# A transformer trunk in which every second weight unit of the down-projection gets its remainder from an adding DMA

## The chip, the cores and the metric

The kernel runs on one core of a Trainium2 chip. The metric is the device time of one execution in microseconds (us), and the median of several runs is compared. Engines are named as in the profile: PE is TensorE (PEld its weight loads), ACT is ScalarE, DVE is VectorE, POOL is GpSimd, and SP is the engine whose queue issues the loads. An engine's name with a q behind it (SPq) is its instruction queue.

## The reference

The reference is a decoder trunk of two layers over 256 tokens of width 2048 in 32-bit floating point. Each layer has an attention mixer with several kinds of heads, a cross-attention into 256 memory tokens, and a squared-ReLU MLP. The change touches the MLP alone, and of that the second product:

```python
def squared_relu_mlp(h, w_up, w_down):          # h (256, 2048)
    return jnp.square(jax.nn.relu(h @ w_up)) @ w_down   # w_up (2048, 8192), w_down (8192, 2048)

for l in range(DEPTH):                          # DEPTH = 2
    ...
    y = squared_relu_mlp(rms_norm(h, g_mlp_pre[l]), w_up[l], w_down[l])
    h = h + rms_norm(y, g_mlp_post[l])
```

## The kernel before

**The split.** Every large product is made from three matmuls. A 32-bit operand is split in two numbers of TensorE's fp32r format: a main part h, which is the operand rounded to fp32r, and a remainder l, which is the operand minus h, rounded likewise. `mm3` adds x_h·w_h, x_h·w_l and x_l·w_h in PSUM.

**Weight units.** Weights stream in from memory in units of two 128-row blocks by up to 512 columns, 512 KB each in the down-projection. A unit goes through three steps. `load` issues its DMA on SP into one of five raw buffers (`RAW = 5`). `convert` writes h on ScalarE (an activation with Copy) and l on VectorE (`tensor_sub` of raw and h), each into one of eight buffers (`WBUF = 8`). `gemm_a` uses h and l on TensorE. A unit of a matrix whose rows are scaled by a gain, the up-projection's among them, is converted in two halves of 512 columns with the gain multiplied in; the down-projection has no gain, so its units take one ScalarE and one VectorE instruction over 1024 elements per partition.

**The MLP.** For each layer, `mlp` runs four quarters q. A quarter has an up stage of four panels of 512 hidden columns (eight units each), whose outputs stay on chip as h and l of the hidden state, and a down stage of four panels of 512 output columns (again eight units each) that multiplies these 2048 hidden values by their rows of w_down and adds the result to y. A panel of the down stage holds two PSUM banks, one for each half of the tokens (tb), and a unit is used by twelve matmuls: two row blocks, two halves, three products. The last panel of the last quarter (q + p == 6) is worked in two passes, first all units for one half of the tokens, then all units for the other, so that the closing norm of the first half can run under the second. Its eight units are therefore in use through both passes.

**Order.** The program order is written out by the generator itself. `pump` places a conversion as soon as fewer than eight units are live, and `feed` places a load as soon as there are fewer than five unconverted ones; `track` keeps a clock for each engine from estimated durations, and these clocks decide where in the program each instruction stands. On the chip every engine runs its own instructions in that order and waits on semaphores: a conversion waits for its raw tile and for TensorE to be done with the unit eight places before, a load waits until the unit five places before has been converted, which is when raw is read no more.

**POOL** converts a few units of other matrices, updates one quarter of the residual at the end of a sub-layer (`UPD_POOL`), and works out some norms.

Of the kernel before, what the change touches and what calls it, by code (L numbers as in the profile page):

```python
# [15 lines left out]
AF = mybir.ActivationFunctionType  # L16
OP = mybir.AluOpType
# [43 lines left out]
class Unit:  # L61
    def __init__(self, dmas, nk, n, gains, passes):
        self.dmas, self.nk, self.n, self.gains, self.left = dmas, nk, n, gains, passes
        self.h = self.l = self.raw = None
        self.pool = False
        self.done_at = None


# [33 lines left out]
def blocks(ap):  # L102

    name = ap.tensor.name
    dims = list(ap.ap)
    o = ap.offset % dims[0][0] if dims[0][0] else ap.offset
    offs = [o]
    for step, num in dims[1:-1]:
        if step >= 64 and num > 1:
            offs = [x + step * i for x in offs for i in range(num)]  # L110
        else:
            dims[-1] = (dims[-1][0], dims[-1][1] + step * num // max(dims[-1][0], 1))
    last = (dims[-1][1] - 1) * dims[-1][0] if len(dims) > 1 else 0
    return {(name, b) for x in offs for b in range(x // 128, (x + last) // 128 + 1)}


class Gen:
# [9 lines left out]

    def __init__(self, ctx, tc, io):
        self.tc, self.nc, self.io = tc, Core(self, tc.nc), io
        self.clk = dict(pe=0.0, act=0.0, dve=0.0, pool=0.0, dma=0.0)  # L130
        self.rd, self.bank = {}, {}
        self.dep = 0.0
        self.seq = 0
        self.heap = []
        self.ready = set()
        self.units = []
        self.nconv = self.ndma = self.ncur = 0
        self.const = ctx.enter_context(tc.tile_pool(name="const", bufs=1))
        self.rawp = ctx.enter_context(tc.tile_pool(name="raw", bufs=self.RAW))
        self.wp = ctx.enter_context(tc.tile_pool(name="w", bufs=self.WBUF))  # L140
        self.xp = ctx.enter_context(tc.tile_pool(name="xt", bufs=4))
        self.tp = ctx.enter_context(tc.tile_pool(name="t", bufs=self.TB))
        self.sp = ctx.enter_context(tc.tile_pool(name="s", bufs=40))
        self.pp = ctx.enter_context(tc.tile_pool(name="ps", bufs=8, space=bass.MemoryType.PSUM))
        ctx.enter_context(tc.manual_schedule())
# [26 lines left out]
    def track(self, part, name, a, k):  # L172
        out = a[0]
        outs = [out] + ([k["accum_out"]] if "accum_out" in k else [])
        ins = [x for x in list(a[1:]) + [v for n, v in k.items() if n != "accum_out"] if isinstance(x, AP)]
        onchip = [x for x in ins if not str(x.space).endswith("DRAM")]
        n = out.free_size() if callable(out.free_size) else out.free_size
        psum = any(str(x.space).endswith("PSUM") for x in onchip)
        lat = 0.12
        if part == "pe":  # L180
            if name == "transpose":
                cost = max(n, 64) * 0.00085
            elif onchip[0].dtype == F32R:
                cost = n * (0.000425 if n >= 256 else 0.0017)
            else:
                cost = max(n, 128) * 0.00168
            lat = 0.2
        elif part == "act":
            cost = (0.03 if psum else 0.06) + n * 0.0009 + 0.093 * ("accum_out" in k) + \
                0.093 * isinstance(k.get("scale"), AP)  # L190
        elif part == "dve":
            if name == "tensor_reduce":
                n = onchip[0].free_size() if callable(onchip[0].free_size) else onchip[0].free_size
            two = 2 if name in ("tensor_scalar", "tensor_copy", "memset") and not psum else 1
            cost = 0.06 + n * 0.00115 / two
        elif part == "pool":
            cost = 0.12 + n * (0.0036 if name == "tensor_scalar" else 0.0023)
            lat = 0.15
        else:
            cost = max(n * 128 * 4 / 350e3, 0.4)  # L200
            lat = 2.0
        start = max([self.clk[part], self.dep] + [self.ready_at(x) for x in onchip])
        if part == "dma":
            start = max(start, self.clk["pe"] - 2.0)
        banks = {x.tensor.name for x in [*onchip, *outs] if str(x.space).endswith("PSUM")}
        for b in banks:
            who, when = self.bank.get(b, (part, 0.0))
            if who != part:
                start = max(start, when)
        end = start + cost  # L210
        self.clk[part] = end
        for b in banks:
            self.bank[b] = (part, end + lat)
        for x in outs:
            for b in blocks(x):
                self.rd[b] = end + lat
# [70 lines left out]
    def convert(self, u):  # L287
        nc = self.nc
        self.seq += 1
        u.h = self.wp.tile([128, 2, 512], F32R, tag="wh", name=f"h{self.seq}")  # L290
        u.l = self.wp.tile([128, 2, 512], F32R, tag="wl", name=f"l{self.seq}")
        n = u.n
        if self.nconv >= self.WBUF:
            self.dep = self.units[self.nconv - self.WBUF].done_at or 0.0
        if u.gains is None:
            a = slice(0, n)
            nc.scalar.activation(u.h[:, :, a], u.raw[:, :, a], AF.Copy)
            (nc.gpsimd if u.pool else nc.vector).tensor_sub(u.l[:, :, a], u.raw[:, :, a], u.h[:, :, a].bitcast(F32))
        else:
            for k in range(u.nk):  # L300
                g = self.gain_col(u.gains[k])
                nc.scalar.activation(u.h[:, k, :n], u.raw[:, k, :n], AF.Copy, scale=g)
                if u.pool:
                    nc.gpsimd.tensor_scalar(u.raw[:, k, :n], u.raw[:, k, :n], g, None, op0=OP.mult)
                    nc.gpsimd.tensor_sub(u.l[:, k, :n], u.raw[:, k, :n], u.h[:, k, :n].bitcast(F32))
                    continue
                nc.vector.scalar_tensor_tensor(u.l[:, k, :n], u.raw[:, k, :n], g, u.h[:, k, :n].bitcast(F32),
                                               op0=OP.mult, op1=OP.subtract)
        u.raw = None
        u.conv_at = self.clk["pool" if u.pool else "dve"]  # L310
        self.dep = 0.0
# [472 lines left out]
    def plan_layer(self, l):  # L784
        io, P = self.io, {}
# [32 lines left out]
        for r in range(0, 32, 4):  # L818
# [4 lines left out]
            u = Unit(d, 2, 512, None, 1)  # L823
# [24 lines left out]
                p.units[i].pool = True  # L848
        for i in self.XO_POOL:
            xo[i].pool = True  # L850
        return P

    UPD_POOL = (3,)
# [709 lines left out]
```

## Time and profile before

| | |
|---|---|
| median of 3 runs | 2479.17 us (2478.69 to 2480.83) |
| the profiled execution, its own time | 2480.92 us |
| its span, first to last instruction | 2479.0 us |
| TensorE busy | 2440.2 us (98%) |
| VectorE busy | 1560.6 us (63%) |
| ScalarE busy | 1334.0 us (54%) |
| POOL busy | 157.6 us (6%) |
| DMA | 447.36 MB, queue of the loads 58.0% of 16 engines |

The span is measured within one profiled execution; the time of the same execution holds a little more (1.9 us here). A busy share is taken over the whole span. Where an engine is idle, the profile names what ended the idle time. Nearly every instruction is issued through one helper, so that all carry the line L84; groups are told apart by engine, operation, shape and the names of the tiles: r is a raw tile, h and l are the parts of a weight unit, t a work tile (the hidden state's parts among them), xt the transposed input, p a PSUM bank, s a small column.

### The profile page before, as it was taken

To read this page: it belongs to the slowest core of one execution; us is meant where nothing else is said; L and a number is where in the kernel's file an instruction comes from. 1 tells how busy PE (TensorE), PEld (TensorE's weight loads), DVE (VectorE), ACT (ScalarE), POOL (GpSimd) and SP (SyncE) were. 2 spreads that over 40 slices of the span, in tenths; PEclk is the share of its full clock that TensorE was granted. 3 is DMA by queue.
4 is the path that set the end of the run, shared out by engine and by line. 5 is a ranking of instruction groups with operands and counts; after the bars stand their busy time and mean duration, and the time that the engine had idled before them with its cause. 6 is when DMAs were issued, how large, how long until landed. Compare 5 with 4: busy or idle time off the path is not lost.

```text
span 2479.0 us, 34733 instructions
## 1 busy us (share of the span) xinstructions
PE 2440.2 (98%) x12803; PEld 2107.4 (85%) x12803; DVE 1560.6 (63%) x2738; ACT 1334.0 (54%) x2283; POOL 157.6 (6%) x266
## 2 busy tenths in 40 slices
PE   8999999999999999999999999999999999999998
PEld 7999999877888888888878989987788888888886
DVE  6855776478646656556666577647864565665665
ACT  7655665467545545445446565646654554544542
POOL 2000000043000000000022000004300000000001
PEclk9999999999999999999999999999999999999999
DMA  8564646545566666566655464654456656666662
GB/s 276 191 175 131 194 118 213 167 153 179 184 197 179 196 195 187 188 195 187 205 160 175 140 189 120 212 177 153 158 185 204 191 186 193 180 198 194 187 207 102
DMA packets 263207, 447.36 MB, mean 180 GB/s; under 512 B 21550, under 2 KB 77566, under 8 KB 263038
## 3 DMA queue, kind: packets, MB, share of 16 engines
q1 hardware_dynamic: 263038, 445.16, 58.0%
q8 instruction: 100, 1.64, 0.3%
q14 instruction: 69, 0.57, 0.1%
HBM read 443.00 MB, written 2.10 MB: 180 GB/s over the span
## 4 chain that ended last, share of the span: by engine, by line
PE 92%; DVE 3%; ACT 2%; POOL 1%; issue 1%; DMA 1%; SPq 0%; POOLq 0%; ACTq 0%; DVEq 0%
PE p L84 92%; DVE l L84 1%; ACT h L84 1%; DVE s L84 1%; DVE t L84 1%; DMA t<-in_x_dram 1%; DVE xt L84 0%; POOL t L84 0%; ACT junk L84 0%; POOL r L84 0%; POOL s L84 0%; ACT t L84 0%; POOL l L84 0%; DMA r<-in_w_in_dram 0%; ACT xt L84 0%
## 5 line engine op out<-in xcount | busy, mean ns | idle before, releaser
L84 PE MATMUL p<-h,t 128*128 128x512 f32 (+2 forms) x3072 | 933.3, 382 | 0.0
L84 DVE SCALAR_TENSOR_TENSOR l<-r,gT,h 128x512 fp32r<-128x512 f32 (+3 forms) x998 | 673.6, 726 | 288.8 <-ACT h L84 286.6
L84 ACT ACTIVATE h<-r,gT 128x512 fp32r<-128x512 f32 (+3 forms) x1008 | 635.2, 687 | 299.6 <-PE p L84 173.9
L84 PE MATMUL p<-xt,h 128*128 128x512 f32 x1920 | 678.9, 399 | 0.0
L84 PEld LDWEIGHTS p<-h,t 128*128 128x128 f32 (+1 forms) x3072 | 565.0, 185 | 109.5
L84 DVE TENSOR_TENSOR l<-r,h 128x1024 fp32r<-128x1024 f32 x346 | 423.4, 1233 | 361.4 <-ACT h L84 359.7
L84 PE MATMUL p<-l,t 128*128 128x512 f32 (+3 forms) x1536 | 584.8, 381 | 0.0
L84 ACT ACTIVATE h<-r 128x1024 fp32r<-128x1024 f32 x352 | 367.5, 1057 | 375.7 <-PE p L84 357.3
L84 PE MATMUL p<-xt,l 128*128 128x256 f32 x1920 | 539.2, 281 | 0.0
L84 PE MATMUL p<-h,xt 128*128 128x384 f32 (+3 forms) x1664 | 501.3, 369 | 1.7 <-ACT h L84 1.6
L84 PEld LDWEIGHTS p<-xt,h 128*128 128x128 f32 x1920 | 360.8, 188 | 89.8
L84 PEld LDWEIGHTS p<-xt,l 128*128 128x128 f32 x1920 | 362.7, 189 | 0.3
L84 PEld LDWEIGHTS p<-h,xt 128*128 128x128 f32 x1664 | 309.7, 189 | 31.6 <-ACT h L84 2.0
L84 PEld LDWEIGHTS p<-l,t 128*128 128x128 f32 (+1 forms) x1536 | 283.6, 185 | 53.7
L84 PE MATMUL p<-l,xt 128*128 128x384 f32 (+3 forms) x832 | 300.8, 362 | 2.6 <-DVE l L84 2.5
L84 ACT ACTIVATE t<-p 128x256 f32<-128x256 f32 (+5 forms) x336 | 140.5, 444 | 101.0 <-PE p L84 98.9
L84 PEld LDWEIGHTS p<-l,xt 128*128 128x128 f32 x832 | 157.5, 189 | 17.1 <-DVE l L84 4.9
L84 POOL TENSOR_SCALAR t<-t,s 128x512 f32<-128x512 f32 x12 | 26.1, 2174 | 2137.6 <-DVE s L84 1716.8
L84 DVE TENSOR_TENSOR t<-p,t 128x256 f32<-128x256 f32 (+3 forms) x220 | 98.0, 473 | 48.8 <-ACT junk L84 29.4
L84 PE MATMUL p<-t,t 128*128 128x128 f32 (+5 forms) x624 | 110.9, 313 | 0.0
L84 PE MATMUL p<-cst,t 128*128 128x128 f32 (+1 forms) x549 | 88.2, 280 | 22.6 <-DVE t L84 12.1
L84 PEld LDWEIGHTS p<-t,t 128*128 128x128 f32 (+3 forms) x624 | 94.8, 195 | 14.4 <-issue 1.3
(77 smaller groups left out, 1129.6 us busy)
## 6 DMA issues: line engine op xcount, KB each, us to landing
r<-in_w_up_dram SPq DMA_DIRECT2D x256, 512.0 KB, 4.2
r<-in_w_down_dram SPq DMA_DIRECT2D x256, 512.0 KB, 4.3
r<-in_w_in_dram SPq DMA_DIRECT2D x96, 384.0 KB, 3.8
r<-in_w_out_dram SPq DMA_DIRECT2D x64, 512.0 KB, 4.1
r<-in_w_in_dram SPq DMA_DIRECT2D x47, 512.0 KB, 4.9
r<-in_w_xkv_dram SPq DMA_DIRECT2D x32, 512.0 KB, 4.4
r<-in_w_xq_dram SPq DMA_DIRECT2D x16, 512.0 KB, 3.7
r<-in_w_xo_dram SPq DMA_DIRECT2D x16, 512.0 KB, 4.0
```

The costliest lines, as they stand in the source:

```text
L84: r = f(*a, **k)
```

## The change

The units of odd number in each panel of the down-projection, 4 of 8 in a panel, 128 of 256 in all, get their remainder otherwise. ScalarE writes h as before. Then ScalarE reads the raw tile a second time with the scale -1 and writes minus the main part into l. A DMA issued from POOL then adds the raw tile onto l in place. The VectorE instruction of these units falls away. The buffer of raw is free when the DMA has landed. In the generator's clocks such a DMA has a part of its own, with the figures 1.0 and 5.0, which serve only to place instructions.

```diff
@@ class Unit
-        self.pool = False
+        self.pool = self.summed = False
@@ Gen.__init__
-        self.clk = dict(pe=0.0, act=0.0, dve=0.0, pool=0.0, dma=0.0)
+        self.clk = dict(pe=0.0, act=0.0, dve=0.0, pool=0.0, dma=0.0, pooldma=0.0)
@@ Gen.track
+        if name == "dma_start" and part == "pool":
+            part = "pooldma"
...
+        elif part == "pooldma":
+            cost, lat = 1.0, 5.0
@@ Gen.convert
             nc.scalar.activation(u.h[:, :, a], u.raw[:, :, a], AF.Copy)
+            if u.summed:
+                nc.scalar.activation(u.l[:, :, a], u.raw[:, :, a], AF.Copy, scale=-1.0)
+                nc.gpsimd.dma_start(u.l[:, :, a], u.raw[:, :, a], accum_op=OP.add)
+                u.raw = None
+                u.conv_at = self.ready_at(u.l)
+                self.dep = 0.0
+                return
             (nc.gpsimd if u.pool else nc.vector).tensor_sub(u.l[:, :, a], u.raw[:, :, a], u.h[:, :, a].bitcast(F32))
@@ Gen.plan_layer
+        for q in range(4):
+            for p in range(4):
+                for u in P["dn", q, p].units[1::2]:
+                    u.summed = True
```

## Rows read from the trace of the kernel before

**Rows 1.** The page, busy time, share of the span and instructions of each engine

```profile
PE 2440.2 (98%) x12803; PEld 2107.4 (85%) x12803; DVE 1560.6 (63%) x2738; ACT 1334.0 (54%) x2283; POOL 157.6 (6%) x266
```

**Rows 2.** Busy time by stage (down, up, down, last down), clock, DMA share

```profile
core 0: us, PE busy (x) PEld busy (x) DVE busy (x) ACT busy (x) POOL busy (x), PEclk, DMA share, GB/s
667.25:754.30 87.05, 87.05 (x386) 72.08 (x385) 44.13 (x46) 41.10 (x50) 0.00 (x0) 1.00 0.63 194
754.30:844.74 90.44, 90.44 (x513) 78.47 (x512) 56.28 (x83) 48.88 (x79) 0.00 (x0) 1.00 0.61 186
844.74:931.81 87.07, 87.07 (x386) 72.08 (x385) 48.06 (x53) 37.38 (x43) 0.00 (x0) 1.00 0.65 194
2381.22:2468.30 87.08, 87.08 (x386) 71.89 (x384) 48.21 (x66) 32.51 (x43) 3.41 (x2) 1.00 0.47 152
```

**Rows 3.** TensorE in a down stage: start, length, instruction, idle before

```profile
699.68 0.61 PE L84 MATMUL p<-h,t 128*128 128x512 f32 x2
...
700.36 0.61 PE L84 MATMUL p<-h,t 128*128 128x512 f32 x2
```

**Rows 4.** ScalarE in order of time in the same stage

```profile
694.66 1.06 ACT L84 ACTIVATE h<-r 128x1024 fp32r<-128x1024 f32 x1 [1.66 <-PE p L84]
697.38 1.06 ACT L84 ACTIVATE h<-r 128x1024 fp32r<-128x1024 f32 x1 [1.66 <-PE p L84]
```

**Rows 5.** VectorE in order of time in the same stage

```profile
695.76 1.23 DVE L84 TENSOR_TENSOR l<-r,h 128x1024 fp32r<-128x1024 f32 x1 [1.49 <-ACT h L84]
698.48 1.23 DVE L84 TENSOR_TENSOR l<-r,h 128x1024 fp32r<-128x1024 f32 x1 [1.49 <-ACT h L84]
```

**Rows 6.** The page, costliest groups: both parts (count, busy, mean ns)

```profile
L84 DVE TENSOR_TENSOR l<-r,h 128x1024 fp32r<-128x1024 f32 x346 | 423.4, 1233 | 361.4 <-ACT h L84 359.7
...
L84 ACT ACTIVATE h<-r 128x1024 fp32r<-128x1024 f32 x352 | 367.5, 1057 | 375.7 <-PE p L84 357.3
```

**Rows 7.** Instructions on raw tiles (least, median, greatest ns); landing of loads

```profile
L84 ACT ACTIVATE h<-r,gT x1008: 598/709/743, 6.5 to 2363.6; 128x512 fp32r<-128x512 f32 x123, 128x384 fp32r<-128x384 f32 x35, 128x448 fp32r<-128x448 f32 x5, 128x396 fp32r<-128x396 f32 x5
...
L84 POOL TENSOR_SCALAR r<-r,gT x10: 1571/2000/2687, 504.7 to 1755.6; 128x512 f32<-128x512 f32 x10
...
DMA to landing us min/median/max: 2.5/4.2/7.6
```

**Rows 8.** What the load queue waited for in that stage: us, times, longest

```profile
SPq L84 <- DVE l L84: 72.8, 32, 6.6
```

**Rows 9.** The page, DMA issues: KB each, median us from issue to landing

```profile
r<-in_w_down_dram SPq DMA_DIRECT2D x256, 512.0 KB, 4.3
```

**Rows 10.** ScalarE at the last down panel of layer 0, then of layer 1

```profile
1262.54 1.06 ACT L84 ACTIVATE h<-r 128x1024 fp32r<-128x1024 f32 x1 [1.66 <-PE p L84]
1265.55 0.63 ACT L84 ACTIVATE junk<-t 128x512 f32<-128x512 f32 x1 [1.95 <-DVE t L84]
...
1267.51 1.05 ACT L84 ACTIVATE h<-r 128x1024 fp32r<-128x1024 f32 x1
...
2448.97 1.04 ACT L84 ACTIVATE h<-r 128x1024 fp32r<-128x1024 f32 x1
```

**Rows 11.** TensorE late in the first pass of the same two panels

```profile
1274.81 0.39 PE L84 MATMUL p<-l,t 128*128 128x512 f32 x1
...
1275.72 0.61 PE L84 MATMUL p<-h,t 128*128 128x512 f32 x2
...
2456.28 0.39 PE L84 MATMUL p<-l,t 128*128 128x512 f32 x1
```

**Rows 12.** Busy time around the change of layers, columns as in group 2

```profile
1250.00:1300.00 50.00, 47.54 (x218) 38.82 (x217) 34.76 (x60) 23.90 (x42) 11.63 (x7) 1.00 0.52 160
1300.00:1350.00 50.00, 48.44 (x230) 40.01 (x229) 31.46 (x67) 34.84 (x70) 15.57 (x62) 1.00 0.51 155
```

**Rows 13.** VectorE behind the last matmul

```profile
2468.49 0.69 DVE L84 TENSOR_TENSOR t<-t,p 128x512 f32<-128x512 f32 x1 [4.85 <-PE p L84]
```

## The prediction

> **What bounds the kernel now.** I read the page's first part, then busy time by stage, then the engines in order of time inside one down stage, then the waits of the load queue. TensorE is busy for 2440.2 of 2479.0 us, VectorE for 63%, ScalarE for 54%, POOL for 6% [rows 1]. The stages say more. In the down stages TensorE is busy from end to end at full clock (87.07 of 87.07 us), while VectorE works 44 to 48 us and ScalarE 33 to 41; POOL does nothing until the last quarter [rows 2]. Three matmuls take 700.36 - 699.68 = 0.68 us [rows 3], so a unit (twelve) takes 2.72 us, and 32 units take 87.04: the stage is TensorE's own work and no wait. ScalarE starts a conversion every 2.72 us, and what it waits for is TensorE's release of a buffer [rows 4]; VectorE follows it and is done 2.33 us after ScalarE began (695.76 + 1.23 - 694.66) [rows 5]. SP waited 72.8 us, over 32 times, for raw tiles to come free [rows 8]. So weights wait for TensorE and not TensorE for weights. The work that is taken from VectorE is off the path that sets the end; what the change can do is make a remainder late.
>
> **What is removed.** 128 instructions of 1.233 us leave VectorE, 157.8 us [rows 6]. They lie beside TensorE's work and are worth 0. In a down stage VectorE goes from 48.06 to about 28 us.
>
> **What is added on ScalarE.** 128 second copies. The plain copy of this size takes 1.057 us [rows 6]; two copies of half the size with a scale, 2 x 0.709 = 1.42 [rows 7], are the upper bound. I take 1.06, since the shape and the constant scale are nearest to the plain copy: 135.7 us in all, 17 per stage, ScalarE from 37.38 to 54.3 of 87.07. They fill part of the 1.66 us in which it waited [rows 4]; cost 0. Behind the copy stand the next h and the emptying of PSUM banks, each at most 1.06 us later; a down panel holds two of eight banks, so a bank has a panel's 21.8 us to spare. If that cover were gone, the cost would be 1.06 us per change of stage, 8.5 in all.
>
> **What is added on POOL.** 128 DMA issues. POOL is idle in the down stages; the norm's steps come after the last issue. The trace has no DMA issued from POOL: an issue costs at least nothing that matters, and the nearest row above is POOL's longest instruction on raw tiles, 2.69 us [rows 7]. One comes every 5.44 us, so both ends fit; 0.
>
> **What is added on the DMA engines.** 128 x 512 KB. The trace has no adding DMA. A plain load: the stage moves 194 GB/s at a share of 0.63 [rows 2], so full engines move 308 GB/s and 512 KB takes 1.70 us of them all. An adding DMA must move its bytes, so it costs at least one such pass, 1.70; it reads raw, reads l and writes l, so three passes, 5.10, is the upper bound. I take two, 3.40: a load too reads and writes, and both are in its one pass, so I count the one further source as one further pass. The stage leaves 0.37 x 87.07 = 32.2 us free, or 2.0 per adding DMA. Beyond that there is stock: the converted units lie 7 x 2.72 - 2.33 = 16.7 us ahead, and a load lands 13.6 - 2.33 - 4.3 = 7.0 us before its turn [rows 5, 9] (five raw buffers, 13.6 us round). The up stage refills it (0.39 x 90.44 = 35 us free). So (32.2 + 16.7 + 7.0) / 16 = 3.49 us is what an adding DMA may take of the engines; 3.40 just fits, 0.
>
> The Trainium skill ("Collectives: The Full Stack", section "The bandwidth ceiling: the fold count and why AG ≠ RS ≠ AR") says that the add itself is free in the DMA, but that it reads two sources and so runs at half the rate of a copy. By that rule this is two passes and the sum stays as it is; by one pass the DMA share would be 0.94 and the stock would not be touched. No run so far shows either.
>
> **What is late next.** Call L the time from the end of ScalarE's second copy to the landing of the sum, POOL's issue included. Before, the remainder was there 1.23 us after h; now it takes 1.06 + L. The least landing of any load is 2.5 us [rows 7]; the upper bound is three loads in a row, 3 x 4.3 = 12.9 [rows 9]. I take 6.0: one landing, 4.3, and the second read's pass, 1.7. Three places wait for it:
> - *The unit itself, in the steady stage.* TensorE comes to it 19.04 us after the conversion began, so L may be 19.04 - 2.12 = 16.9. Nothing.
> - *The raw buffer.* The next load must land 13.6 us after the start: L up to 7.2 costs no delay at all. Five is odd, so a buffer holds summed and plain units by turns: (2.12 + L + 4.3) + (2.33 + 4.3) must stay under 27.2, so the rate holds to L = 14.1. SP's queue has the following loads behind the wait, but these have stock. Nothing.
> - *The two-pass panel, once per layer.* Its first pass takes a unit every 1.36 us, so the lead is short. ScalarE converts the last unit, an odd one, at 1267.51 to 1268.56, held up by the squares at 1265.55 [rows 10]. The second copy ends at 1269.62. TensorE wants that unit's l at 1274.81 [rows 11]. In the second layer the times are 2448.97 + 1.04 + 1.06 = 2451.07 and 2456.28. So L may be 5.2 us; beyond that TensorE stands still, with nothing to cover it. At L = 6.0 this is 0.8 us a layer, 1.6 in all. (Unit 5 of the panel begins 7.7 us earlier and has L up to 10.2.)
>
> **The sum.** 0 + 0 + 0 + 0 + 1.6 us. The profiled execution took 2480.9 us with a span of 2479.0; the median of the runs is 2479.2, which I take as base. **2480.8 us, no change that can be measured.** A difference under 0.2% (5.0 us) cannot be told from none in this kernel.
>
> The Trainium skill ("DMA: Bandwidth & Descriptors", section "Anatomy of one DMA — SWDGE (gpsimd) path") gives a DMA issued from POOL about 2.0 us fixed plus the bytes at 436 GB/s, 3.2 us for 512 KB, an estimate that does not include an add. By that alone L is under 5.2 and the sum would be 2479.2. No run so far has such a DMA.
>
> **Rivals.**
> - *The two-pass panel stalls in earnest (slower).* It decides from L = 7.7, where 2 x (L - 5.2) passes 5.0 us. At 12.9 it costs 15.4: 2494.6. For it: the load's own greatest landing is 7.6 [rows 7], and in the first layer loads of the next layer run beside it. Against it: in the second layer nothing loads any more at that point, and the share of the last stage is 0.47 [rows 2].
> - *The DMA engines become the bound (slower).* It decides from 3.49 us of all engines per adding DMA. At three passes, (5.10 - 3.49) x 16 x 8 stages = 206 us: 2685. At 4.0, 65 us: 2544. For it: the share is already 0.63 while the stage lasts. Against it: the loads' time on the engines holds their reading from memory, which transfers inside the core do not do.
> - *POOL's issuing is the pace (slower).* It decides from 5.44 + 16.9/16 = 6.5 us per issue. At 7.0, 16 x 1.56 - 16.9 = 8.1 us a stage: 2544. Against it: nothing of POOL on these tiles takes over 2.69.
> - *ScalarE's second copy delays bank or hidden state (slower):* 8.5 us, 2487.7, if no bank were spare. Against it: TensorE has no idle time at the changes of stage in [rows 2].
> - *VectorE's relief shortens the handovers (faster).* TensorE is idle for 2.46 + 1.56 = 4.0 us around the change of layers [rows 12]; if all of it came back, 2475.2, still within 0.2%. Behind the last matmul VectorE had been idle for 4.85 us [rows 13], so the tail gains nothing. Only a reordered program could give more.
> - *The change does not do what it says* would mean that VectorE keeps its 1560.6 us; nothing speaks for that, and the time would be the base.
>
> **How the numbers follow.** No measurable change, L below 7.7 and passes that fit: 0.56. The stalled panel 0.19, the DMA engines 0.13, POOL 0.04, ScalarE 0.04, faster 0.04. Slower together 0.40. The predicted time is that of the likeliest case; its own range is 2475 to 2484. The whole range goes from 2475, the most that the handovers can give back, to 2540, which takes in the stalled panel and ScalarE whole and the DMA case while its cost stays below 4.0 us; what is left out is most of the DMA and POOL cases and half of the faster one, 0.17.
>
> **What would show it.** VectorE at about 1403 us and ScalarE at about 1470, with 128 DMAs from POOL, show the parts. Down stages of 87.07 us show that neither engines nor POOL set the pace; a stage that is longer, with a DMA share near 1, the DMA rival, and with POOL's issues back to back, POOL's. A gap of TensorE ahead of an l of the last panel's last unit, waiting for a DMA, shows L: the gap is L - 5.2. The prediction is wrong if that gap exceeds 2.5 us, or if a stage grows by over 0.4 us.

## The result, and the profile after

The changed kernel takes 2501.83 us (median of 3 runs, 2501.32 to 2503.43) where the kernel before takes 2479.17: the ratio is 1.0091, 95% interval 1.0068 to 1.0114. It is slower by 22.7 us, inside the range, in the direction to which I gave 0.40. The likeliest case, no measurable change, did not come.

The page of the changed kernel, first its engines, then its DMA queues (the new one is q0, the DMAs that POOL issues), then groups, then issues:

```profile
PE 2444.9 (98%) x12803; PEld 2108.9 (84%) x12803; DVE 1405.6 (56%) x2610; ACT 1444.8 (58%) x2411; POOL 268.4 (11%) x394
...
q1 hardware_dynamic: 263038, 445.16, 55.3%
q0 software_dynamic: 18432, 67.12, 13.9%
...
L84 PE MATMUL p<-l,t 128*128 128x512 f32 (+3 forms) x1536 | 586.9, 382 | 16.1 <-DMA l<-r 16.1
...
L84 ACT ACTIVATE h<-r 128x1024 fp32r<-128x1024 f32 x352 | 367.0, 1053 | 315.4 <-DMA r<-in_w_down_dram 194.1
...
L84 POOL DMA_DIRECT2D l<-r x128 | 110.8, 865 | 1218.8 <-ACT l L84 1133.1
...
L84 ACT ACTIVATE l<-r 128x1024 fp32r<-128x1024 f32 x128 | 133.4, 1042 | 0.0
...
r<-in_w_down_dram SPq DMA_DIRECT2D x256, 512.0 KB, 6.8
l<-r POOLq DMA_DIRECT2D x128, 512.0 KB, 7.0
```

Against [rows 1, 6, 9] VectorE has lost 155 us and ScalarE and POOL have gained 111 each. Two things are new: TensorE has 16.1 us of idle time ahead of matmuls that use l, ended by an adding DMA, and ScalarE's h now waits for loads of w_down, while in the kernel before it waited for TensorE [rows 4, 6]. A load of w_down lands in 6.8 us where it took 4.3.

The stages again, two ordinary down stages and the last of each layer (span of the stage; busy PE, PEld, DVE, ACT, POOL; clock, DMA share, GB/s):

```profile
667.57:754.62 87.05, 87.05 (x387) 72.07 (x386) 28.21 (x33) 52.01 (x63) 11.22 (x13) 1.00 0.99 281
1022.56:1109.63 87.07, 87.07 (x387) 72.08 (x385) 32.14 (x40) 48.36 (x56) 11.25 (x13) 1.00 1.00 282
1200.07:1297.90 97.83, 88.97 (x387) 71.95 (x386) 37.16 (x59) 51.37 (x68) 14.75 (x15) 0.98 0.88 241
2392.10:2489.00 96.90, 88.98 (x385) 72.60 (x384) 32.73 (x53) 44.03 (x56) 14.71 (x15) 0.98 0.81 220
```

The ordinary stages have kept their length, 87.05 and 87.07 us as in [rows 2], though the DMA engines are now full (0.99 and 1.00 for 0.63). All the lost time lies in the last down stage of each layer. In the second layer VectorE took up the last matmul's result 2468.49 - 2381.22 = 87.27 us after the stage's begin [rows 13, 2]; now TensorE ends its last run of matmuls at 2489.50 (below), 97.4 us after it. What ScalarE waited for in the first down stage, which lost nothing, shows what had changed already there (us, times, longest):

```profile
ACT h L84 <- DMA r<-in_w_down_dram: 20.6, 9, 3.8
ACT h L84 <- PE p L84: 5.0, 4, 2.7
```

In the kernel before, in the same stage, none of its waits was for a load; the greatest was this one:

```profile
ACT h L84 <- PE p L84: 38.3, 25, 1.7
```

What TensorE waited for over the whole span, the one line on sums:

```profile
PE p L84 <- DMA l<-r: 16.1, 7, 5.1
```

Seven gaps, and all of them lie in the last quarters: four in the first layer (8.2 us), three in the second (7.9). The chain of work behind the longest, in the second layer (start, length, what):

```profile
2448.33 4.75 DMA l<-r
...
2453.10 0.37 SPq L84
...
2453.56 10.40 DMA r<-in_w_down_dram
...
2464.04 1.07 ACT h L84
2465.13 1.23 DVE l L84
2466.36 0.61 DVE t L84
2466.99 1.30 DVE t L84 x2
...
2469.10 0.95 ACT h L84
2470.05 0.95 ACT l L84
...
2471.35 4.43 DMA l<-r
...
2475.82 13.68 PE p L84 x53
```

Read it downward: an earlier sum lands at 2453.08 and with that frees a raw buffer, SP issues a load into it, the load takes 10.4 us, then ScalarE and VectorE on that unit (the seventh of the two-pass panel), then VectorE's emptying of two PSUM banks, which stands behind this conversion in its queue, then the squares, and only then ScalarE's two copies for the eighth unit, the adding DMA, and TensorE at 2475.82, after 5.08 us without work. The copies of that unit begin 2469.00 - 2392.10 = 76.9 us after the stage's begin. In the kernel before they began at 2448.97, 67.75 us after it [rows 10, 2]. From the end of the second copy (2470.99) to TensorE's matmul are 4.8 us: the sum itself was not late, its conversion was.

Behind the two longest gaps the granted clock fell. ScalarE's last copy and TensorE in order of time in the first layer, and the granted clock there (the last three figures: clock, DMA share, GB/s):

```profile
1279.28 1.04 ACT L84 ACTIVATE l<-r 128x1024 fp32r<-128x1024 f32 x1
```

```profile
1279.92 0.50 PE L84 MATMUL p<-l,t 128*128 128x512 f32 x1 [4.44 <-DMA l<-r]
...
1280.81 0.63 PE L84 MATMUL p<-l,t 128*128 128x512 f32 x1
1281.24 1.05 PE L84 MATMUL p<-h,t 128*128 128x512 f32 x2
...
1285.96 0.50 PE L84 MATMUL p<-l,t 128*128 128x512 f32 x1 [1.43 <-DMA l<-r]
```

```profile
1278.00:1282.00 4.00, 2.08 (x6) 1.69 (x7) 0.89 (x5) 2.31 (x4) 0.86 (x1) 0.83 0.73 216
1282.00:1286.00 4.00, 2.57 (x8) 1.66 (x7) 0.00 (x0) 0.00 (x0) 0.00 (x0) 0.75 0.86 206
```

The matmul at 1280.81 is followed by the next after 0.43 us, where they followed each other in 0.227. The granted clock says 0.83 and 0.75 for these two stretches, so for some 3.4 us (0.17 x 4 + 0.25 x 4 = 1.7 us, at half the rate) TensorE ran at 1.2 of its 2.4 GHz; before that it had stood still for 4.44 us. In the second layer the same 1.7 us follow the gap of 5.08. Gaps and lower clock together, 16.1 + 2 x 1.7 = 19.5, make up most of the 21.0 us by which the span grew. As a cause the clock counts in the second layer alone: in the first, TensorE next waited for the sum of the last unit, whose second copy had ended at 1280.32, before the clock fell, so at full clock that wait of 1.43 us would have been longer by as much.

### The profile page after: what moved, and what is told of

It is laid out like the page before. It is cut to its first block, busy times and chain, and to the rows that moved or that the text cites. A ratio compares the mean times of both kernels' runs of the same rounds, so it can differ in the third digit from the quotient of the medians.

```text
span 2500.0 us, 35035 instructions
## 1 busy us (share of the span) xinstructions
PE 2444.9 (98%) x12803; PEld 2108.9 (84%) x12803; DVE 1405.6 (56%) x2610; ACT 1444.8 (58%) x2411; POOL 268.4 (11%) x394
## 3 DMA queue, kind: packets, MB, share of 16 engines
q1 hardware_dynamic: 263038, 445.16, 55.3%
q0 software_dynamic: 18432, 67.12, 13.9%
## 4 chain that ended last, share of the span: by engine, by line
PE 84%; DMA 5%; DVE 4%; issue 3%; ACT 2%; POOL 2%; SPq 0%; POOLq 0%; ACTq 0%; DVEq 0%
PE p L84 84%; DMA l<-r 2%; DMA r<-in_w_down_dram 2%; DVE l L84 2%; ACT h L84 1%; DVE s L84 1%; POOL s L84 1%; DVE t L84 1%; DMA t<-in_x_dram 1%; DVE xt L84 0%; POOL t L84 0%; ACT junk L84 0%; POOL r L84 0%; ACT t L84 0%; POOL l L84 0%
## 5 line engine op out<-in xcount | busy, mean ns | idle before, releaser
L84 PE MATMUL p<-l,t 128*128 128x512 f32 (+3 forms) x1536 | 586.9, 382 | 16.1 <-DMA l<-r 16.1
L84 DVE TENSOR_TENSOR l<-r,h 128x1024 fp32r<-128x1024 f32 x218 | 269.0, 1238 | 530.8 <-ACT h L84 529.2
L84 ACT ACTIVATE h<-r 128x1024 fp32r<-128x1024 f32 x352 | 367.0, 1053 | 315.4 <-DMA r<-in_w_down_dram 194.1
L84 PEld LDWEIGHTS p<-l,t 128*128 128x128 f32 (+1 forms) x1536 | 284.3, 185 | 72.7 <-DMA l<-r 19.0
L84 POOL DMA_DIRECT2D l<-r x128 | 110.8, 865 | 1218.8 <-ACT l L84 1133.1
L84 ACT ACTIVATE l<-r 128x1024 fp32r<-128x1024 f32 x128 | 133.4, 1042 | 0.0
```

The source lines that it names most:

```text
L84: r = f(*a, **k)
```

## The experiments

Each is timed beside the kernel before on the same chip; the ratio and its 95% interval are against it. The kernel before had medians of 2479.3 to 2479.9 us there. Two theories stood at the start. By the **stock theory** the sums fill the DMA engines, loads come late, the stock of converted units is used up, and the two-pass panel is where this shows. By the **landing theory** the sums of that panel are late by themselves.

**Sums in the two-pass panel alone.**

```diff
-                    u.summed = True
+                    u.summed = q == 3 and p == 3
```

> Only the odd units of the two-pass panel (last panel of the last quarter) are summed, 8 adding DMAs in all. Stock theory (the adding DMAs fill the DMA engines through the whole down stage, loads come late, the stock of converted units is used up, and the two-pass panel, which takes units at twice the pace, is where it shows): the engines are not full before the panel, so its sums land in about 4.8 us, as the very last one of the changed kernel did, under the 5.2 us that there are; 2479 to 2481 us. Landing theory (the time from the second copy to the landing, 7.0 us in the median, is by itself too long for the short lead of that panel): the gaps of TensorE stay, 2483 us at least and up to the 2502 of the full change.

Measured: 2480.39 us, ratio 1.0001 (0.9992 to 1.0010); TensorE never waits for a sum. Busy time of the 22 us ahead of that panel, with the clock, DMA share and GB/s at the end:

```profile
1243.00:1265.00 22.00, 22.00 (x99) 18.22 (x98) 8.86 (x11) 12.56 (x15) 2.79 (x3) 1.00 0.75 207
```

A share of 0.75 leaves room, and the sums are in time. In the same 22 us of the changed kernel the engines were full:

```profile
1243.00:1265.00 22.00, 20.82 (x92) 16.94 (x91) 7.48 (x8) 14.16 (x17) 4.33 (x5) 1.00 1.05 294
```

The share is a sum of packet times and comes out a little over 1 here. The landing theory, that the sums of this panel are late with free engines too, falls.

**Sums everywhere but there.**

```diff
-                    u.summed = True
+                    u.summed = not (q == 3 and p == 3)
```

> All odd units of the down-projection are summed except those of the two-pass panel, 120 adding DMAs. Stock theory: the engines are full until that panel begins and its loads are still late, but four sums of 2.7 us fall away inside it; part of the loss stays, 2483 to 2495 us. Landing theory: no summed unit is left where the lead is short; 2479 us.

Measured: 2480.58 us, ratio 1.0006 (0.9997 to 1.0015). The stock theory's 2483 is missed as well, though what it says of the loads is there. ScalarE at the two-pass panel, and the same 22 us as above:

```profile
1263.70 1.06 ACT L84 ACTIVATE h<-r 128x1024 fp32r<-128x1024 f32 x1 [2.63 <-DMA r<-in_w_down_dram]
1267.16 1.06 ACT L84 ACTIVATE h<-r 128x1024 fp32r<-128x1024 f32 x1 [2.40 <-DMA r<-in_w_down_dram]
1268.49 1.06 ACT L84 ACTIVATE h<-r 128x1024 fp32r<-128x1024 f32 x1 [0.27 <-DMA r<-in_w_down_dram]
```

```profile
1243.00:1265.00 22.00, 22.00 (x98) 17.90 (x97) 9.14 (x11) 11.50 (x14) 1.72 (x2) 1.00 0.93 267
```

The engines are nearly full (0.93) and three conversions in a row wait for loads; and still TensorE waits for only 0.49 us, once, for the last unit's l, since the remainder made by VectorE follows h within 1.3 us. So neither theory holds alone. Late loads and slow sums have to meet in the panel that takes a unit every 1.36 us. This **joint theory** is what the next runs test.

**Sums in quarters 0 to 2.**

```diff
-                    u.summed = True
+                    u.summed = q < 3
```

> Summed units in quarters 0 to 2 only, 96 adding DMAs. Stock theory: each of these stages ends with its stock low but is followed by an up stage that refills it, and no panel of them takes units at double pace; 2479 to 2480 us. Landing theory: the same, 2479. A third theory, that every adding DMA costs a little everywhere, would leave three quarters of the 22.7 us: 2496.

Measured: 2480.18 us, ratio 1.0002 (0.9993 to 1.0011). 96 of the 128 sums cost nothing that can be told; the third theory falls.

**Every fourth unit.**

```diff
-                for u in P["dn", q, p].units[1::2]:
+                for u in P["dn", q, p].units[3::4]:
```

> Units 3 and 7 of each panel are summed, 64 adding DMAs. Stock theory: a stage needs 54.8 us of the engines for loads and 8 x 2.71 = 21.7 for sums, 76.5 of 87, so loads stay on time; 2479 to 2482 us. Landing theory: the last unit of the two-pass panel, with the shortest lead, is still summed, so its gap stays; 2483 to 2490.

Measured: 2480.19 us, ratio 1.0004 (0.9995 to 1.0013). With half the sums the engines keep pace: over the whole span ScalarE waits 5.4 us for loads of w_down, where it waited 194.1. The last unit, summed as before, is in time.

**The last panel in one pass**, without and with sums. The panel is worked as the others, and both closing norms follow it. (The run without sums also sets `u.summed = False`.)

```diff
-                P["dn", q, p] = self.plan(..., passes=2 if q + p == 6 else 1)
+                P["dn", q, p] = self.plan(..., passes=1)
...
-                if q == 3 and p == 3:
+                if False:
...
+                    if q == 3 and p == 3:
+                        for tb in range(2):
+                            self.part_mean(ssq[tb], r2[:, 2 + tb:3 + tb])
                     b = self.gemm_a(P["dn", q, p], hlhs)
                     for tb in range(2):
                         evac(tb, p, b[tb])
+                        if q == 3 and p == 3:
+                            self.spawn(self.chain(tb, y[tb], ssq[tb], XT, self.rs, self.ep, r2, late=8.0))
+                            self.run_side()
```

> The kernel before, with the last down panel of the last quarter worked in one pass for both halves of the tokens, as the other panels are (nothing summed). It is the base for the next run. Both closing norms now start behind the panel, so the time rises by up to the 11 us of half a panel per layer: 2480 to 2500 us.

> The changed kernel with the same one-pass panel. Joint theory (the stock, used up by full DMA engines, and the summed units of the two-pass panel at double pace are needed together): units are taken every 2.72 us to the end, the stock lasts, and this run is at most 3 us above the one-pass base. If the double pace were not part of the cause, some 20 us would stay between the two.

Measured: 2494.31 us without sums (ratio 1.0064, 1.0052 to 1.0076) and 2503.02 with them (1.0094, 1.0081 to 1.0107). The difference is 8.7 us; I expected 3 at most. What TensorE waited for, with sums and then without (us, times, longest):

```profile
PE p L84 <- DVE t L84: 19.4, 13, 10.4
...
PE p L84 <- DMA l<-r: 1.2, 2, 0.7
```

```profile
PE p L84 <- DVE t L84: 14.0, 13, 5.0
```

The waits for sums have gone from 16.1 us to 1.2, as the joint theory says. But a wait for VectorE's t at the change of layers has grown from 5.0 to 10.4 us. In VectorE's queue the closing norm stands behind conversions of the next layer's first units, and with sums the loads of these are late. ScalarE at the last conversion ahead of the norm, with sums and then without:

```profile
1286.67 1.33 ACT L84 ACTIVATE h<-r,gT 128x512 fp32r<-128x512 f32 x2 [1.44 <-DMA r<-in_w_in_dram]
```

```profile
1281.77 1.34 ACT L84 ACTIVATE h<-r,gT 128x512 fp32r<-128x512 f32 x2 [1.38 <-PE p L84]
```

The longer wait and the waits for sums, 5.4 + 1.2, are 6.6 of the 8.7 us. So late loads find another way to TensorE where the pace is even, through the order of VectorE's queue.

**Small adds.**

```diff
-                nc.gpsimd.dma_start(u.l[:, :, a], u.raw[:, :, a], accum_op=OP.add)
+                nc.gpsimd.dma_start(u.l[:, :, 0:64], u.raw[:, :, 0:64], accum_op=OP.add)
```

> The changed kernel, but each of the 128 adding DMAs covers 64 of 512 columns, an eighth of the bytes; the rest of the remainder stays at minus the main part (left out: seven eighths of the sum). All steps, waits and issues stay. Joint theory: the engines are not full, share about 0.70 in a down stage, loads land in 4.3 us; 2479 to 2481 us. If the loss came from the steps themselves (the second copy on ScalarE, the issue on POOL, the one more wait), 2490 to 2502 us would stay.

Measured: 2479.56 us, ratio 1.0004 (0.9995 to 1.0012). The first down stage:

```profile
667.60:754.60 87.00, 87.00 (x387) 72.09 (x386) 27.34 (x31) 54.27 (x65) 15.71 (x13) 1.00 0.74 211
```

All the steps are there, VectorE's relief is there (27 us busy for 44), and the time is that of the kernel before. The share is 0.74. Steps and relief together change nothing that can be told. Every engine's instructions stand in the order of the changed kernel, so the order is not the cause either.

This run also parts two things that full engines do at once: a load takes longer, and a raw buffer is held longer, because the sum reads it. What the load queue waited for over the whole span, in the changed kernel and then with small adds:

```profile
SPq L84 <- DMA l<-r: 455.2, 123, 7.0
```

```profile
SPq L84 <- DMA l<-r: 489.6, 124, 7.6
```

Loads waited for small adds at least as long as for whole ones, and no time was lost. So raw buffers that are held until a DMA lands are not enough; the engines' time is needed.

**All units.**

```diff
-                for u in P["dn", q, p].units[1::2]:
+                for u in P["dn", q, p].units[:]:
```

> All 256 units of the down-projection are summed. The page of the changed kernel gives 13.9% of 16 engines' span for 128 sums, 2.71 us of all engines each. Engine theory: a stage needs 54.8 us for loads and 32 x 2.71 = 86.7 for sums, 141.5, against 87.1 and a stock of 23.7 (16.7 of converted units and 7.0 of loads): 31 us a stage, 246 in all, 2725 us, with a share near 1 throughout the down stages. If the sums only cost where the lead is short, both two-pass panels lose twice what they lost: about 2525 us.

Measured: 2727.06 us, ratio 1.0996 (1.0982 to 1.1010), beside the 2725 that the sum over the engines gave. Its DMA queues, and 87 us of the first down stage:

```profile
q1 hardware_dynamic: 263038, 445.16, 49.2%
q0 software_dynamic: 36864, 134.23, 25.5%
```

```profile
667.00:754.00 87.00, 72.74 (x294) 54.85 (x293) 4.19 (x8) 47.35 (x55) 19.85 (x23) 0.98 1.04 265
```

25.5% of 2719.2 us over 256 sums is 2.71 us each once more, and the engines are full through the stage, in which TensorE works 72.7 of 87 us.

**A panel without sums ahead of the two-pass one, or three panels ahead.**

```diff
-                    u.summed = True
+                    u.summed = not (q == 3 and p == 0)      # skip_p0
+                    u.summed = not (q == 3 and p == 2)      # skip_p2
```

> All odd units are summed except those of the first panel of the last quarter, 120 adding DMAs. Joint theory: a panel with sums needs 8 x 1.70 + 4 x 2.71 = 24.4 us of the engines in 21.8, so each takes 2.7 us from the stock, which is full when the last quarter's down stage begins and stays full over a panel without sums; two panels instead of three draw on it before the two-pass panel, 5.4 us instead of 8.0. Most of the loss stays but not all: 2485 to 2497 us. If the place made no difference and only the number of sums counted, 120/128 of 22 us: 2500.

> All odd units are summed except those of the third panel of the last quarter, the one ahead of the two-pass panel, 120 adding DMAs. Joint theory: that panel needs 13.6 us of the engines in 21.8 and gives the stock back (8.2 us free against 5.4 taken), so the two-pass panel begins as in the run with its sums alone; 2479 to 2483 us. If only the number counted, 2500.

Measured: 2489.69 us (1.0044, 1.0030 to 1.0058) without sums in the first panel, 2484.25 (1.0018, 1.0009 to 1.0027) without them in the third. By the ratios, of the 22.7 us some 11 and 4.5 are left. So the same eight sums are worth about 12 us of the loss in the first panel, 18 in the third, and 21 in the two-pass panel itself (1.0006 left). The number of sums does not decide, their place does. The second is over the 2483 that I allowed: in the two-pass panel ScalarE still waits for late loads (3.58 us at one conversion in the first layer, 4.12 in the second), and TensorE for the last sum, 2.40 and 2.90 us. One panel does not quite give the stock back.

**A copy in place of the add.**

```diff
-                nc.gpsimd.dma_start(u.l[:, :, a], u.raw[:, :, a], accum_op=OP.add)
+                nc.gpsimd.dma_start(u.l[:, :, a], u.raw[:, :, a])
```

> The changed kernel with a DMA of the same bytes from the same queue that copies raw over l in place of adding (left out: the sum; l is then the raw weight). It measures the pass without the second read. If an add counts as two passes, the copy takes half of the 2.71 us per DMA, 1.35; a stage then needs 76.4 of 87 us and the time is 2479 to 2482. If an add costs the engines no more than a copy, 2.71 stays and so does the loss, 2495 to 2502.

Measured: 2480.93 us, ratio 1.0006 (0.9997 to 1.0015). Its queue on the page:

```profile
q0 software_dynamic: 18432, 67.12, 7.8%
```

Its DMAs: issue on POOL (ns least, median, greatest) and landing (us least, median, greatest):

```profile
L84 POOL DMA_DIRECT2D l<-r x128: 527/527/777, 653.1 to 2450.5; - x128
...
DMA to landing us min/median/max: 2.8/5.5/7.5
```

And the landing of the adding DMAs in the changed kernel:

```profile
DMA to landing us min/median/max: 4.4/7.0/9.9
```

7.8% of 2478.2 us over 128 is 1.51 us of all engines for a copy; an add takes 2.71, 1.8 times as much, lands 1.5 us later, and takes POOL 0.86 us to issue instead of 0.53. With copies the loss is gone.

**Two small adds in a chain, in the two-pass panel alone.**

```diff
-                    u.summed = True
+                    u.summed = q == 3 and p == 3
...
-                nc.gpsimd.dma_start(u.l[:, :, a], u.raw[:, :, a], accum_op=OP.add)
+                for _ in range(2):
+                    nc.gpsimd.dma_start(u.l[:, :, 0:64], u.raw[:, :, 0:64], accum_op=OP.add)
```

> Only the odd units of the two-pass panel are summed, and there by two small adding DMAs one after the other, each over 64 of 512 columns (left out: the rest of the sum; the columns that are added get raw twice). The engines stay free, so the stock is full, and only the landing is late: 0.3 us plus twice a small add of at least 2.7 and in the median of the run with small adds 5.3 us, 6 to 11 us. It tests the price that the prediction put on this place, 2 x (L - 5.2): 2481 to 2491 us, with a gap of TensorE of L - 5.2 at the panel's last unit in each layer. Joint theory in the form that the lead is lost only through full engines, and not through the landing: 2479 to 2480.

Measured: 2484.10 us, ratio 1.0015 (1.0006 to 1.0024). ScalarE's copies for the last unit in the first layer, and TensorE's matmul that waited:

```profile
1270.07 1.05 ACT L84 ACTIVATE h<-r 128x1024 fp32r<-128x1024 f32 x1
1271.02 1.04 ACT L84 ACTIVATE l<-r 128x1024 fp32r<-128x1024 f32 x1
```

```profile
1278.40 0.47 PE L84 MATMUL p<-l,t 128*128 128x512 f32 x1 [0.86 <-DMA l<-r]
```

The second copy ends at 1272.06, TensorE goes on at 1278.40: L is 6.3 us and the gap 0.86, where L - 5.2 is 1.1. In the second layer the gap is 0.90. The gaps come out near the price that the prediction put on this place, as long as the stock is full; together they are 1.8 us, and the time rose by some 4 (1.5 to 6.0 by the interval). So late landing alone can cost time there too, from about 5.5 us on (6.34 - 0.86). The plain add of the run with sums in this panel alone was only just in time: in the first layer TensorE took the last unit's l at 1275.13, 5.5 us after the second copy had ended at 1269.61.

## Why the prediction was right, and where it was not

The time lies inside the range because the range was wide, up to 2540 for a part of the DMA rival; no single case that was worked out gives 2501.8. The prediction's own sign of being wrong came in both its parts: it allowed a gap of 2.5 us and a stage longer by 0.4 us, and the gaps were 4.44 and 5.08 us, the last stages about 10 us longer. Step by step:

**VectorE** (157.8 us off, worth 0): 155 us off, worth 0; in the run with small adds it is off as well, and the time is that of the kernel before.

**ScalarE** (128 x 1.06 us, worth 0): the copies take 1.042 us each; together the engine's busy time grew by 111 us and not 136, since each of two neighbouring copies begins some 0.1 us before the one ahead of it ends. Worth 0: the ordinary stages kept their length.

**POOL** (between 0 and 2.69 us an issue, worth 0): 0.865 us, worth 0.

**The DMA engines** (1.70 to 5.10 us per sum, taken as 3.40, "just fits, 0"): 2.71, between one pass and two. 3.49 as the point from which an ordinary stage grows was on the right side: at 2.71 none did. With all units summed the same sum of passes, free engines and stock gave 2725 us, and 2727 was measured. The rule of the Trainium skill ("Collectives: The Full Stack", section "The bandwidth ceiling: the fold count and why AG ≠ RS ≠ AR"), stated there for the collective ReduceScatter, that an add reads two sources and runs at half a copy's rate nearly holds here: an add took 1.8 times the copy's 1.51 us.

**The landing** (L = 6.0): 7.0 from the issue in the changed kernel, with full engines; 4.8 from the second copy for the very last sum, which had the engines to itself. The formula in the Trainium skill ("DMA: Bandwidth & Descriptors", section "Anatomy of one DMA — SWDGE (gpsimd) path") gives an estimate of 3.2 us for a plain DMA of this size; no run had one on idle engines. The plain copy took 5.5 beside the loads and 2.8 at the least, which is under the estimate; the measurement decides.

**The two-pass panel** (2 x (L - 5.2) = 1.6 us): this is the step that failed. Its place was right, and the run with two small adds finds gaps near its price. But I worked out the 5.2 from the times at which the kernel before converts that panel's units, and in the step just ahead I had let the sums use up the stock that these times stand for ("3.40 just fits, 0"). A panel with sums needs 8 x 1.70 + 4 x 2.71 = 24.4 us of the engines in its 21.8, so by this count three panels take 8 us from the 23.7; and the panel that then takes units at twice the pace had its last conversion 9 us late in the second layer (76.9 us after the stage's begin for 67.75). The terms were each worth 0 or little alone, as the two runs with the one or the other alone show (1.0001 and 1.0006), and together 22.7 us. Added to it is the lower clock behind the longest gap, 1.7 us in the second layer, which I had not counted.

Of the **rivals**, the stalled panel came in its place and at more than its 15.4 us, but not by its condition: it was to need L above 7.7, and ahead of the longest gap L was 4.8. What was late was the conversion, because the engines were full, which was the next rival and did not set the pace of an ordinary stage. Against the stalled panel I had said that in the second layer nothing loads any more at that point; now one of the panel's own loads ran until 2463.96. POOL's pace, ScalarE's delay, the handovers and the change without effect did not come.

**What stays open**: raw buffers held by a DMA are not enough by themselves (the run with small adds), but how much the longer hold adds once the engines are full was not separated; a sum's landing does stand ahead of the late load in the chain above. No run followed the stock from panel to panel, so the 8 us are an estimate. And of the last 1.5 of the 21.0 us, 1.3 are busy time of TensorE (2444.9 for 2440.2, less 3.4 for the clock), with no cause found.

## What to carry to other kernels

A stock that hides one cost must not be counted again as cover for the next: write down what each step draws from it, and look for the place that draws fastest, here a panel that takes units at twice the pace. Work that is moved off an engine which nobody waits for brings nothing, while what replaces it can be free in three quarters of its places and still lose time in the fourth. An adding DMA of this kind should be counted on the DMA engines as nearly two copies (1.8 here).

## What the runs showed of the hardware that I had not expected

A load's time on the engines fell as they filled: the queue of the loads took 58.0% of 2479.0 us before, 1438 us, then 55.3% of 2500.0, 1383, and 49.2% of 2719.2, 1338, with all units summed, for the same 263038 packets. One reading is that part of a load's packet time with free engines is time in which others can be served; no run tests it.

The small adds of 64 columns took POOL 1.20 us to issue, more than the whole ones' 0.86, for an eighth of the bytes (34816 packets in all against 18432).
